# Expert lookup of a two-block transformer layer: experts in token-block order, routing placed between the row products

## Chip, cores, metric

One core of a Trainium2 chip runs the whole program. The metric is the device time of one execution in microseconds (us); the kernel before took 1429.31 us (median of 3 runs, 1425.92 to 1430.74).

## What is computed

Two blocks of a model run on 256 tokens of width 1024. All but the last stage (a mixer of attention, a recurrence and a convolution, twice; then a second block with its own mixers) is left alone by the change. The last stage is `peer`, a product-key mixture of 16384 experts, 8 heads, 16 experts per head and token:

```python
def one(xb):                                     # xb: a block of 128 tokens
    q = (xb @ w_pq).reshape(PEER_BLOCK, PEER_HEADS, 2, PEER_DKH)
    s = jnp.einsum('thpd,hpkd->thpk', q, sub_keys).astype(jnp.float32)
    sv, si = lax.top_k(s, PEER_TOPK)
    cand = (sv[:, :, 0, :, None] + sv[:, :, 1, None, :]).reshape(PEER_BLOCK, PEER_HEADS, -1)
    cidx = (si[:, :, 0, :, None] * N_KEYS + si[:, :, 1, None, :]).reshape(PEER_BLOCK, PEER_HEADS, -1)
    best, pos = lax.top_k(cand, PEER_TOPK)
    eidx = jnp.take_along_axis(cidx, pos, axis=-1)
    g = jax.nn.softmax(best, axis=-1)
    act = jax.nn.gelu(jnp.einsum('thkd,td->thk', expert_u[eidx], xb).astype(jnp.float32), approximate=False)
    return jnp.einsum('thk,thkd->td', (g * act).astype(xb.dtype), expert_v[eidx])
```

Its result, times a gate vector, is added to the residual and is the output.

## The kernel before

The program is written as a list of engine instructions; a scheduler turns it into one fixed order per engine at build time. `at(us)` sets the priority of what follows (lower goes first), but whatever is ready in the scheduler's own estimate may go ahead. On the chip each engine then runs its list in that order and waits where an operand or a buffer isn't ready. Tiles come from pools: `mk(..., tag, bufs=n)` means that n buffers of that name go round, and a new one waits for the release of an old one.

`peer` works on the two token blocks b = 0, 1 (128 tokens each, one per partition) and the heads h = 0 to 7:

- `scores(h)`: two weight tiles of 512 KB come in (`wpq`, issued on SP's queue), each is split by ACT into a rounded part `wh` (L323) and by DVE into the rest `wl` (L268), PE multiplies (48 matmuls), ACT copies the result to `qs` (L1480), and 4 matmuls give `sp`, a PSUM tile of the scores of both blocks. There are three buffers each for `wh` and `wl`, and two for `sp`.
- `routing(h, b)`: some 28 small DVE instructions, all in a chain: the top 16 of two rows of 128 scores (`top16`, L1464 to L1469, which reads `sp` in PSUM), 256 sums `cand`, their top 16, and from the positions the expert numbers `eix` (one-hot rows `oh`, a sum `ij`, L1521). ACT makes the exponentials of the softmax (L1526) in the middle; DVE then needs its sum for a reciprocal (L1527).
- `experts(h, b)`: for each of 16 experts POOL issues one gather (L1556): 128 rows of 8 KB, one per token, holding both `expert_u` and `expert_v`, into a buffer `G` of 8 KB per partition. DVE makes the row product (L1559): `G` times `hn[b]`, summed over 1024 columns. After a chunk of `CH` = 4 experts ACT applies Gelu (L1561), DVE multiplies with the softmax weights into `w` (L268), ACT makes four diagonal matrices `dg` (L1566, three buffers), and PE adds each expert's second half to two PSUM accumulators per block (`c`, `o` for block 0, `t`, `acx` for block 1). When PE has read a `G`, its buffer is free for another gather. There are `NG` = 11 of them.
- ACT loads a table whenever it goes from Gelu to the exponential or back.
- Eight more weight tiles (`wada`) are summed on DVE into `gs` (L262, `modsum`) for the gate vector `gtb`. At the end DVE multiplies the accumulators with it and adds the residual, and four transfers write the output.

Order of work before: head by head, block 0 then block 1 of each head (`for h ... for b ...: experts(h, b, ...)`). All calls of `scores` and `routing` stand ahead of the experts in the program with priorities spread over the stage; the scheduler takes them as soon as they are ready.

Of the kernel before, what the change touches and what calls it, by code (L numbers as in the profile page):

```python
# [240 lines left out]
def program(tc, A, dbg=lambda *a: None, stop=99):  # L241
# [1200 lines left out]
    def peer(B):  # L1442
# [17 lines left out]
        gat = [mk(pp, [128, 8, 16], tag=f"gat{b}") for b in range(2)]  # L1460
        io16 = C("iota")[:, None, 0:16].broadcast_to([128, 32, 16])

        def top16(v, ix, src, n):
# [4 lines left out]
            dve.max(v[:, 8:16], w)
            dve.max_index(ix[:, 8:16], v[:, 8:16], w)  # L1469

        def scores(h, t):
# [13 lines left out]
            return sp  # L1485
# [11 lines left out]
        def routing(h, b, sp):  # L1497
# [15 lines left out]
            sif = mk(pp, [128, 2, 16], tag="sif", bufs=2)
            dve.tensor_copy(sif, si)
            oh = mk(pp, [128, 2, 16, 16], tag="oh", bufs=1)
            of = oh.rearrange("p w k c -> p (w k) c")
            tt(of, io16, pf.rearrange("p w k -> p (w k)")[:, :, None].broadcast_to([128, 32, 16]), ALU.is_equal)
            for w in range(2):
                tt(oh[:, w], oh[:, w], sif[:, w, None, :].broadcast_to([128, 16, 16]), mul)
            ij = mk(pp, [128, 2, 16], tag="ij", bufs=2)  # L1520
            dve.tensor_reduce(ij.rearrange("p w k -> p (w k)"), of, axis=AX.X, op=add)  # L1521
            stt(eix[b][:, h], ij[:, 0], 128.0, ij[:, 1], mul, add)
# [19 lines left out]
        CH = 4  # L1542
        vacc = []

        def experts(h, b, t):
# [3 lines left out]
            for c in range(0, 16, CH):  # L1549
# [26 lines left out]
        for b in range(2):  # L1576
            routing(0, b, sps[0])
# [68 lines left out]
```

## Time and profile before

| | |
|---|---|
| median of 3 runs | 1429.31 us |
| the profiled execution: its own time / span in the profile | 1432.05 us / 1430.3 us |
| busy: PE / DVE / ACT / POOL | 86% / 69% / 36% / 21% of the span |
| gathers (queue q0): bytes, share of the 16 DMA engines | 268.45 MB, 46.0% of the span |
| mean granted TensorE clock | 0.924 |

The span runs from the first to the last instruction. The profile cuts it into 40 slices of 35.8 us; `peer` takes the last 20 of them (the first gather is issued at 725.8 us). "Idle before" of an instruction names what ended the wait. A DMA's time to landing is counted from its issue. PEclk is the clock granted to TensorE, 1.00 for 2.4 GHz and 0.50 for 1.2 GHz.

### The profile page before, as it was taken

The page shows a single profiled execution, that of the slowest core. Times are in us where ns is not written, and L with a number is a line of the kernel's source. Part 1 is how long each engine was busy: PE and PEld are TensorE (multiplying, and loading weights), DVE is VectorE, ACT ScalarE, POOL GpSimd, SP SyncE. Part 2 cuts the span into 40 slices and gives each one's busy share as a digit, 9 for nine tenths or more (in the row PEclk, how much of TensorE's full clock was granted, in tenths as well). Part 3 has the DMA queues.
Part 4 walks back from the last instruction along what each step waited for, and adds up shares of the span by engine and source line. Part 5 has one row for each costly group of instructions (what it writes and reads, how often), then busy time and mean ns, then how long its engine had stood idle before and what let it go on. Part 6 is the DMA issues. An engine that isn't in the chain of part 4 may idle for free.

```text
span 1430.3 us, 17866 instructions
## 1 busy us (share of the span) xinstructions
PE 1226.4 (86%) x6050; PEld 805.5 (56%) x6050; DVE 981.7 (69%) x2452; ACT 519.0 (36%) x1116; POOL 307.3 (21%) x279
## 2 busy tenths in 40 slices
PE   6999899999889999999897677788787877878786
PEld 5988568789759888658785333333333333333332
DVE  6898855699977673556689999955555545455554
ACT  5536643445755553454533334311111111111111
POOL 0000000000000000000032344454454444434450
PEclk9999999899999997989998789899999899998999
DMA  8677547556314341401379799999999999999994
GB/s 322 202 273 259 176 136 249 162 171 231 118 38 129 123 126 59 133 0 45 133 313 422 273 350 344 372 420 422 422 422 421 422 421 422 421 421 421 422 421 201
DMA packets 71339, 387.50 MB, mean 271 GB/s; under 512 B 8401, under 2 KB 9425, under 8 KB 38226
## 3 DMA queue, kind: packets, MB, share of 16 engines
q0 software_dynamic: 36864, 268.45, 46.0%
q1 hardware_dynamic: 34386, 117.93, 24.5%
q8 instruction: 48, 0.79, 0.2%
q14 instruction: 41, 0.34, 0.1%
HBM read 385.30 MB, written 1.05 MB: 270 GB/s over the span
## 4 chain that ended last, share of the span: by engine, by line
PE 48%; DMA 21%; DVE 14%; issue 9%; POOL 5%; ACT 2%; POOLq 0%; SPq 0%; DVEq 0%; ACTq 0%
PE acc L256 22%; DMA G<-uv,eix 18%; PE acx L256 10%; PE s L256 5%; DVE G L1559 5%; POOL G L1556 5%; PE t L256 2%; DMA wm<-wada 2%; PE o L256 2%; PE c L963 2%; DVE oh L268 1%; PE s L412 1%; PE c L256 1%; PE t L259 1%; DVE tmp L1467 1%
## 5 line engine op out<-in xcount | busy, mean ns | idle before, releaser
L1559 DVE SCALAR_TENSOR_TENSOR G<-G,hn 128x1024 f32<-128x1024 f32 x256 | 313.9, 1227 | 224.9 <-DMA G<-uv,eix 215.3
L1556 POOL DMA_INDIRECT G<-uv,eix x256 | 300.0, 1172 | 393.3 <-PE o L256 146.3
L323 ACT ACTIVATE wh<-w 128x1024 fp32r<-128x1024 f32 (+2 forms) x142 | 148.6, 1048 | 204.3 <-PE acc L256 124.9
L268 DVE TENSOR_TENSOR wl<-w,wh 128x1024 fp32r<-128x1024 f32 (+2 forms) x142 | 171.7, 1212 | 62.7 <-ACT wh L323 61.7
L256 PE MATMUL t<-G,dg 128*128 128x512 f32 x256 | 150.0, 671 | 68.5 <-ACT dg L1566 68.5
L256 PE MATMUL c<-G,dg 128*128 128x512 f32 x256 | 147.9, 662 | 65.0 <-ACT dg L1566 65.0
L256 PE MATMUL acc<-hh,wh 128*128 128x256 f32 x608 | 178.6, 297 | 7.9 <-ACT hh L468 3.6
L256 PE MATMUL acc<-hh,wl 128*128 128x256 f32 x608 | 180.4, 299 | 2.0 <-DVE wl L268 2.0
L256 PE MATMUL acc<-hl,wh 128*128 128x256 f32 x608 | 168.3, 291 | 3.7 <-issue 2.1
L1566 ACT ACTIVATE dg<-cst,w 128x128 f32<-128x128 f32 x256 | 89.8, 394 | 161.4 <-PE acx L256 72.7
L256 PE MATMUL acx<-G,dg 128*128 128x512 f32 x256 | 143.5, 645 | 0.0
L256 PE MATMUL o<-G,dg 128*128 128x512 f32 x256 | 142.5, 641 | 0.0
L256 PEld LDWEIGHTS t<-G,dg 128*128 128x128 f32 x256 | 51.3, 211 | 146.5 <-ACT dg L1566 91.8
L1561 ACT ACTIVATE s<-s 128x4 f32<-128x4 f32 x64 | 13.2, 205 | 326.4 <-DVE G L1559 326.4
L256 PEld LDWEIGHTS acc<-hh,wh 128*128 128x128 f32 x608 | 121.5, 200 | 14.5 <-issue 4.5
L256 PEld LDWEIGHTS c<-G,dg 128*128 128x128 f32 x256 | 50.5, 209 | 139.9 <-ACT dg L1566 88.4
L256 PEld LDWEIGHTS acc<-hh,wl 128*128 128x128 f32 x608 | 122.1, 201 | 9.6 <-issue 5.2
L256 PEld LDWEIGHTS acc<-hl,wh 128*128 128x128 f32 x608 | 116.0, 197 | 5.8 <-issue 3.4
L262 DVE SCALAR_TENSOR_TENSOR g<-lu,pb,g 128x256 f32<-128x256 f32 x264 | 115.7, 483 | 0.2
L256 PEld LDWEIGHTS acx<-G,dg 128*128 128x128 f32 x256 | 53.7, 210 | 71.1 <-issue 71.1
L256 PEld LDWEIGHTS o<-G,dg 128*128 128x128 f32 x256 | 53.0, 207 | 69.9 <-issue 69.9
L1054 POOL MEMSET lu<- 128x16 f32 x1 | 0.2, 180 | 400.5 <-ACT onat L840 400.5
(493 smaller groups left out, 2003.3 us busy)
## 6 DMA issues: line engine op xcount, KB each, us to landing
w<-w SPq DMA_DIRECT2D x64, 512.0 KB, 5.4
wm<-wada SPq DMA_DIRECT2D x40, 512.0 KB, 4.2
wa<-cw SPq DMA_DIRECT2D x16, 512.0 KB, 4.1
w<-woa SPq DMA_DIRECT2D x16, 512.0 KB, 3.4
w<-wpq SPq DMA_DIRECT2D x16, 512.0 KB, 3.3
w<-w2t SPq DMA_DIRECT2D x12, 512.0 KB, 3.5
w<-wob SPq DMA_DIRECT2D x8, 512.0 KB, 4.3
w<-w2v SPq DMA_DIRECT2D x8, 512.0 KB, 3.8
```

The source lines that it names most:

```text
L256: pe.matmul(out, lhsT, rhs, start=start, stop=stop)
L259: pe.transpose(out, in_, ident)
L262: (e or dve).scalar_tensor_tensor(out, a, s, b, op0=op0, op1=op1)
L268: return (e or dve).tensor_tensor(out, a, b, op=op)
L323: act.activation(hi, w, AF.Copy)
L412: pe.matmul(acc[j:j + 32], ones[:, 0:32], sq[:, q] if square else srcs[i + q], start=i + q < 4, stop=i + q >= n - 4, tile_position=(0, j))
L963: pe.matmul(acc[32 * j:32 * j + 32], sc[:, k], w[:, j], start=k == 0, stop=k == 7, tile_position=(0, 32 * j))
L1467: dve.match_replace(w, v[:, 0:8], src, -3e38)
L1556: pool.indirect_dma_start(out=G, out_offset=None, in_=A["uv"], in_offset=bass.IndirectOffsetOnAxis(ap=eix[b][:, h, c + j:c + j + 1], axis=0))
L1559: dve.scalar_tensor_tensor(G[:, 0:D], G[:, 0:D], 1.0, hn[b], op0=mul, op1=mul, accum_out=s[:, j:j + 1])
L1561: act.activation(s, s, AF.Gelu)
L1566: act.activation(dg, ident, AF.Copy, scale=w[:, j:j + 1])
```

## The change

1. Experts go block by block: round r = 0 to 15 is head r % 8 of block r // 8.
2. `routing` becomes a generator that gives out one instruction at a time. Round r is given the routing of round r + 2 (round 0 those of rounds 1 and 2), and behind each row product `nside` of its instructions are pinned on DVE: 2, in round 0 4. Only `routing(0, 0)` runs ahead of the first gather.
3. `scores` copies its result from PSUM to `sca`, an SBUF tile for all heads (16 KB per partition), with one more ACT instruction per head; `routing` reads that. `scores(r + 2)` stands with round r.
4. The sums for the gate vector go in the same way from round 3 on; the output of block 0 from round 10 on, in a buffer of `G`; that of block 1 at the end.
5. The last round's chunks are 4, 4, 4, 2, 1, 1 rather than four of 4.
6. `NG` goes from 11 to 9, `cand` from two buffers to one, `PICK` (spacing of the priorities) from 2.6 to 2.5.

```diff
-        def routing(h, b, sp):
+        def routing(h, b):
+
+            def top16(v, ix, src, n):
+                w = mk(pp, [128, n], tag="tmp", bufs=2)
+                yield dve.max(v[:, 0:8], src)
...
-                top16(sv[:, p], si[:, p], sp[:, b, p], 128)
...
+                yield from top16(sv[:, p], si[:, p], sca[:, h, b, p], 128)
...
-            return sp
+            act.activation(sca[:, h], sp, AF.Copy)
...
+                    dot = dve.scalar_tensor_tensor(G[:, 0:D], G[:, 0:D], 1.0, hn[b], op0=mul, op1=mul,
+                                                   accum_out=s[:, j:j + 1])
                     rows.append(G)
...
+                    with tc.issue_after(dot.ins):
+                        for _ in range(nside):
+                            while side and next(side[0], 0) == 0:
+                                side.pop(0)
...
-        PICK, NG = 2.6, 11
+        PICK, NG = 2.5, 9
...
+        for r in range(16):
+            nxt = [routing(q % 8, q // 8) for q in ((1, 2) if r == 0 else (r + 2,)) if q < 16]
+            side[0:0] = nxt
+            if r == 3:
+                side.append(gate_sums())
+            if r == 10:
+                side.append(finish(0))
+            if r < 6:
+                scores(r + 2, U0 + 16 * PICK * r - 12)
+            experts(r % 8, r // 8, U0 + 16 * PICK * r, 4 if r == 0 else 2, (4, 4, 4, 4) if r < 15 else (4, 4, 4, 2, 1, 1))
+            at(U0 + 16 * PICK * (r + 1))
+            while side and (side[0] in nxt or r in (6, 12)):
+                for _ in side.pop(0):
+                    pass
```

How it stands on DVE. First, two row products that follow each other among the first 16 experts of the kernel before (the product is the row with `hn`; `eix`, `best`, `sv`, `si`, `pos` and `gat` belong to routing, `gs` to the gate sums):

```order
L1559 SCALAR_TENSOR_TENSOR G_8616,s_8609<-G_8616,hn_1231_7173 128x1024
L262 SCALAR_TENSOR_TENSOR eix_1233_7175<-ij_7630 128x16
L1468 MAX best_7654<-tmp_7658 128x8
L1468 MAX sv_7749<-tmp_7753 128x8
L262 SCALAR_TENSOR_TENSOR gs_8476<-w_8491,sc_19_102,gs_8476 128x1024
L1465 MAX_INDEX si_7750<-sv_7749,s_7744 128x8
L1469 MAX_INDEX pos_7655<-best_7654,tmp_7658 128x8
L265 TENSOR_SCALAR gat_1236_7178<-best_7654 128x16
L1469 MAX_INDEX si_7750<-sv_7749,tmp_7753 128x8
L1559 SCALAR_TENSOR_TENSOR G_8619,s_8609<-G_8619,hn_1231_7173 128x1024
```

and of the kernel after, in round 1:

```order
L1562 SCALAR_TENSOR_TENSOR G_7830,s_7829<-G_7830,hn_1231_7173 128x1024
L1497 MAX sv_7789<-tmp_7803 128x8
L1498 MAX_INDEX si_7790<-sv_7789,tmp_7803 128x8
L1562 SCALAR_TENSOR_TENSOR G_7835,s_7829<-G_7835,hn_1231_7173 128x1024
L268 TENSOR_TENSOR cand_7838<-sv_7789 128x256
L1494 MAX best_7840<-cand_7838 128x8
L1562 SCALAR_TENSOR_TENSOR G_7844,s_7829<-G_7844,hn_1231_7173 128x1024
L1495 MAX_INDEX pos_7841<-best_7840,cand_7838 128x8
L1496 MATCH_REPLACE tmp_7842<-best_7840,cand_7838 128x256
L1562 SCALAR_TENSOR_TENSOR G_7849,s_7829<-G_7849,hn_1231_7173 128x1024
```

Eight instructions, of three routings and of the gate sums, stood between two products; now there are two of one routing.

Second, DVE just ahead of the first gather, which needs `eix`, in the kernel before (`wl` are the splits for later heads, `ij` the last sum ahead of `eix`):

```order
L268 TENSOR_TENSOR wl_7686<-w_7682,wh_7684 128x1024
L1469 MAX_INDEX si_7291<-sv_7290,tmp_7300 128x8
L268 TENSOR_TENSOR cand_7304<-sv_7290 128x256
L268 TENSOR_TENSOR oh_7278<-oh_7278,sif_7276 128x256 x2
L1514 CAST sif_7319<-si_7291 128x32
L1464 MAX best_7306<-cand_7304 128x8
L268 TENSOR_TENSOR wl_7716<-w_7712,wh_7714 128x1024
L1521 TENSOR_REDUCE ij_7282<-oh_7278 128x32
L1464 MAX sv_7441<-s_7436 128x8
L1465 MAX_INDEX pos_7307<-best_7306,cand_7304 128x8
L1467 MATCH_REPLACE tmp_7310<-best_7306,cand_7304 128x256
L262 SCALAR_TENSOR_TENSOR eix_1233_7175<-ij_7282 128x16
```

and after:

```order
L268 TENSOR_TENSOR oh_7280<-cst_62,pf_7276 128x512
L268 TENSOR_TENSOR wl_7464<-w_7460,wh_7462 128x1024
L1529 RECIPROCAL sm_7288<-sm_7288 128x1
L268 TENSOR_TENSOR oh_7280<-oh_7280,sif_7278 128x256 x2
L265 TENSOR_SCALAR gat_1235_7177<-gat_1235_7177,sm_7288 128x16
L1523 TENSOR_REDUCE ij_7284<-oh_7280 128x32
L268 TENSOR_TENSOR wl_7721<-w_7717,wh_7719 128x1024
L262 SCALAR_TENSOR_TENSOR eix_1233_7175<-ij_7284 128x16
```

The other routings are gone from this stretch; two splits still stand ahead of `eix`.

Third, the end of DVE's list before, from the last chunk but one on (`w` is the chunk's weights, `t` and `acx` the accumulators of block 1):

```order
L268 TENSOR_TENSOR w_2182_10511<-s_10497,gat_1236_7178 128x4
L1559 SCALAR_TENSOR_TENSOR G_10530,s_10529<-G_10530,hn_1232_7174 128x1024
L1559 SCALAR_TENSOR_TENSOR G_10533,s_10529<-G_10533,hn_1232_7174 128x1024
L1559 SCALAR_TENSOR_TENSOR G_10536,s_10529<-G_10536,hn_1232_7174 128x1024
L1559 SCALAR_TENSOR_TENSOR G_10539,s_10529<-G_10539,hn_1232_7174 128x1024
L268 TENSOR_TENSOR w_2192_10543<-s_10529,gat_1236_7178 128x4
L268 TENSOR_TENSOR G_10561<-t_8511,gtb_8475 128x512
```

and after:

```order
L268 TENSOR_TENSOR w_2184_10527<-s_10513,gat_1236_7178 128x4
L1562 SCALAR_TENSOR_TENSOR G_10546,s_10545<-G_10546,hn_1232_7174 128x1024
L1562 SCALAR_TENSOR_TENSOR G_10549,s_10545<-G_10549,hn_1232_7174 128x1024
L268 TENSOR_TENSOR w_2192_10553<-s_10545,gat_1236_7178 128x2
L1562 SCALAR_TENSOR_TENSOR G_10564,s_10563<-G_10564,hn_1232_7174 128x1024
L268 TENSOR_TENSOR w_2197_10568<-s_10563,gat_1236_7178 128x1
L1562 SCALAR_TENSOR_TENSOR G_10575,s_10574<-G_10575,hn_1232_7174 128x1024
L268 TENSOR_TENSOR w_2201_10579<-s_10574,gat_1236_7178 128x1
L268 TENSOR_TENSOR G_10585<-t_7500,gtb_7425 128x512
```

The last four experts had one `w` behind all of them; now the first two have one, and the last two one each.

## Rows read from the trace of the kernel before

**Rows 1.** Page, part 2: busy tenths of DVE in 40 slices, and GB/s.

```profile
DVE  6898855699977673556689999955555545455554
...
GB/s 322 202 273 259 176 136 249 162 171 231 118 38 129 123 126 59 133 0 45 133 313 422 273 350 344 372 420 422 422 422 421 422 421 422 421 421 421 422 421 201
```

**Rows 2.** Windows of `peer`: from:to, us, busy (x instructions), clock, DMA share, GB/s.

```profile
728.00:780.00 52.00, 44.59 (x261) 35.88 (x259) 46.46 (x149) 17.57 (x30) 20.03 (x18) 0.93 1.01 418
780.00:920.00 140.00, 102.12 (x212) 44.72 (x212) 138.14 (x514) 52.82 (x106) 57.32 (x44) 0.82 0.88 333
920.00:1408.00 488.00, 386.04 (x790) 158.98 (x791) 253.67 (x450) 80.45 (x250) 220.76 (x194) 0.92 1.01 421
```

**Rows 3.** Groups by line and form, 780 to 920 us: DVE and POOL.

```profile
L1559 DVE SCALAR_TENSOR_TENSOR G<-G,hn 128x1024 f32<-128x1024 f32 x45 | 55.6, 1238 | 0.0
L268 DVE TENSOR_TENSOR oh<-cst,pf 128x512 f32<-128x512 f32 x12 | 8.6, 713 | 0.0
L262 DVE SCALAR_TENSOR_TENSOR gs<-w,sc,gs 128x1024 f32<-128x1024 f32 x6 | 8.1, 1348 | 0.0
L1556 POOL DMA_INDIRECT G<-uv,eix x44 | 58.8, 1336 | 86.5 <-PE acx L256 18.5 <-PE o L256 14.3 <-DVE ij L1521 13.6
```

**Rows 4.** Waits, longest in total first: of 780 to 920 us, then of 920 to 1400 us.

```profile
ACT gat L1526 <- DVE gat L265: 31.0, 8, 12.6
...
DVE G L1559 <- DMA G<-uv,eix: 209.2, 181, 1.7
```

**Rows 5.** DVE, POOL and ACT in order of time ahead of the first row product.

```profile
707.76 0.60 ACT L1480 ACTIVATE qs<-acc 128x512 f32<-128x512 f32 x1 [1.82 <-PE acc L256]
...
710.48 0.29 DVE L1464 MAX8 sv<-s 128x8 f32<-128x128 f32 x1
...
725.34 0.18 DVE L262 SCALAR_TENSOR_TENSOR eix<-ij 128x16 uint32<-128x16 f32 x1
...
725.81 1.08 POOL L1556 DMA_INDIRECT G<-uv,eix  x1 [20.38 <-DVE eix L262]
727.19 1.01 POOL L1556 DMA_INDIRECT G<-uv,eix  x1 [0.30 <-issue]
```

**Rows 6.** All gathers, line L1556: durations, and time from issue to landing.

```profile
L1556 POOL DMA_INDIRECT G<-uv,eix x256: 932/938/2275, 725.8 to 1397.8; - x128
...
DMA to landing us min/median/max: 6.7/16.1/17.1
```

**Rows 7.** DVE in order of time, one chunk of the later part: a chunk's last product, the weights behind it.

```profile
1292.98 1.23 DVE L1559 SCALAR_TENSOR_TENSOR G<-G,hn 128x1024 f32<-128x1024 f32 x1 [1.27 <-DMA G<-uv,eix]
...
1294.49 0.16 DVE L268 TENSOR_TENSOR w<-s,gat 128x4 f32<-128x4 f32 x1 [0.27 <-ACT s L1561]
...
1302.93 1.23 DVE L1559 SCALAR_TENSOR_TENSOR G<-G,hn 128x1024 f32<-128x1024 f32 x1 [1.26 <-DMA G<-uv,eix]
```

**Rows 8.** PE in order of time: a chunk at full clock, then the start of one at the lower.

```profile
1285.24 1.13 PE L256 MATMUL c<-G,dg 128*128 128x512 f32 x2 [2.82 <-ACT dg L1566]
...
1291.35 1.02 PE L256 MATMUL o<-G,dg 128*128 128x512 f32 x2
1295.20 2.07 PE L256 MATMUL c<-G,dg 128*128 128x512 f32 x2 [2.82 <-ACT dg L1566]
...
1301.80 1.02 PE L256 MATMUL c<-G,dg 128*128 128x512 f32 x2
```

**Rows 9.** Windows of 4 us: first and last of 17 dips of the clock after 940 us.

```profile
984.00:988.00 4.00, 3.33 (x4) 1.51 (x5) 1.94 (x4) 0.99 (x3) 0.00 (x0) 0.50 1.01 422
1376.00:1380.00 4.00, 4.00 (x6) 1.54 (x5) 2.37 (x4) 0.57 (x2) 1.13 (x1) 0.57 1.01 420
```

**Rows 10.** The end, in order of time: last product, Gelu, first and last matmul pair, last addition.

```profile
1414.24 1.23 DVE L1559 SCALAR_TENSOR_TENSOR G<-G,hn 128x1024 f32<-128x1024 f32 x1 [1.23 <-DMA G<-uv,eix]
...
1416.46 1.13 PE L256 MATMUL t<-G,dg 128*128 128x512 f32 x2 [3.97 <-ACT dg L1566]
...
1424.27 1.02 PE L256 MATMUL acx<-G,dg 128*128 128x512 f32 x2
1424.47 0.69 DVE L268 TENSOR_TENSOR G<-t,gtb 128x512 f32<-128x512 f32 x1 [8.56 <-PE t L256]
```

More of the change, by code (lines that the diff above doesn't have):

```diff
@@ L1505, in routing @@
             best = mk(pp, [128, 16], tag="best", bufs=2)
             pos = mk(pp, [128, 16], U32, tag="pos", bufs=2)
-            top16(best, pos, cand.rearrange("p a b -> p (a b)"), 256)
+            yield from top16(best, pos, cand.rearrange("p a b -> p (a b)"), 256)
             pi = mk(pp, [128, 2, 16], U32, tag="pi", bufs=2)
-            ts(pi[:, 0], pos, 4, None, ALU.logical_shift_right)
-            ts(pi[:, 1], pos, 15, None, ALU.bitwise_and)
+            yield ts(pi[:, 0], pos, 4, None, ALU.logical_shift_right)
@@ L1518, in routing @@
             for w in range(2):
[L1519 removed]
+                yield tt(oh[:, w], oh[:, w], sif[:, w, None, :].broadcast_to([128, 16, 16]), mul)
             ij = mk(pp, [128, 2, 16], tag="ij", bufs=2)
[L1521 to L1522 removed]
+            yield dve.tensor_reduce(ij.rearrange("p w k -> p (w k)"), of, axis=AX.X, op=add)
@@ L1523, in routing @@
+            yield stt(eix[b][:, h], ij[:, 0], 128.0, ij[:, 1], mul, add)
             g = gat[b][:, h]
-            ts(g, best, best[:, 0:1], None, sub)
+            yield ts(g, best, best[:, 0:1], None, sub)
             sm = mk(pp, [128, 1], tag="sm", bufs=2)
             act.activation(g, g, AF.Exp, accum_out=sm)
-            dve.reciprocal(sm, sm)
-            ts(g, g, sm, None, mul)
+            yield dve.reciprocal(sm, sm)
+            yield ts(g, g, sm, None, mul)
         xn = XT.rearrange("p k t -> p (k t)").rearrange("p (b d) -> p b d", b=2)
@@ L1569, in experts @@
                            h == 7 and c + j == 15)
-        PICK, NG = 2.6, 11
+                c += n
+        PICK, NG = 2.5, 9
         U0 = B + 22
-        sps = {}
-        sps[0] = scores(0, B)
+        scores(0, B)
         at(B + 8)
-        for b in range(2):
-            routing(0, b, sps[0])
+        for _ in routing(0, 0):
+            pass
         at(B + 5.5)
         natural()
-        for h in range(1, 8):
-            sp = scores(h, U0 + 32 * PICK * (h - 1) - 8)
-            for b in range(2):
-                at(U0 + 32 * PICK * (h - 1) + 6 + 16 * PICK * b)
-                routing(h, b, sp)
+        scores(1, B + 9)
         at(B + 16)
```

84 lines of the change are left out of this document (44 added, 40 removed).

## The prediction

> **What bounds the kernel now.** I read the page's slices first. In the last 20 of 40 slices the kernel gathers experts: from slice 27 on it moves 420 to 422 GB/s in every slice but the last, which is the transfers' own limit, while DVE is half busy. Four slices ahead of that (23 to 26) show 273 to 372 GB/s with DVE at 9 tenths [rows 1]. The windows give sizes. From 728 us on, when gathers are under way, 418 x 52 + 333 x 140 + 421 x 488 = 21.7 + 46.6 + 205.4 = 273.8 MB are moved in 680 us; at 421 GB/s they take 650 us. Nearly all of the difference lies in 780 to 920 us: 46.6 MB want 110.7 us and took 140, so **29.3 us are lost there** [rows 2].
>
> Who loses them is seen in the groups and waits of that stretch. DVE works 138.1 of 140 us [rows 2] and gets through 45 row products, where a gather every 2.49 us (a chunk of four takes 1302.93 - 1292.98 = 9.95 us [rows 7]) would ask for 56. Besides the products it did 12 routings and 6 gate sums [rows 3]. The chain behind a product is ACT, PE, and then POOL, which has no free buffer: ACT waited 31.0 us, once 12.6 us, for a routing's softmax on DVE, with the Gelu of a chunk queued behind it; PE then has no diagonal matrices, frees no `G`, and POOL issues nothing. After 920 us, when all routing is done, it is the products that wait for gathers, 209.2 us in all [rows 4]: the transfers set the pace.
>
> So the stage has a floor: first issue, plus 650 us of transfers, plus a tail. The change can save the 29.3 us, part of the start and part of the tail, and can lose by making the transfers wait anew.
>
> **Routing between the products.** It is all kept, only spread. In the crowded stretch 138.1 - 55.6 (products) - 8.1 (sums) leaves 74.4 us for 12 routings, 6.2 us each [rows 2, 3]. A round takes 16 x 2.49 = 39.8 us and now holds 16 x 1.24 = 19.8 us of products, 6.2 us of routing and four `w` of 0.16 us [rows 3, 7]: 27 us, 67%. In early rounds two splits of a weight tile come on top (1024 columns, so about a product each, 2.5 us), in rounds 3 to 6 two gate sums each (2.7 us [rows 3]), still below 33 us. Round 0 holds two routings and more splits, about 36 us. DVE therefore keeps up everywhere, and two routing instructions (the longest, 0.71 us [rows 3]) behind a product fit in the 1.25 us that DVE is idle ahead of the next one [rows 7]. The lost 29.3 us go: **-29.3**.
>
> **New waits on DVE.** The reciprocal and the last multiplication of a routing stand in DVE's list with products behind them, and wait for ACT's exponential, which stands behind other ACT work. The trace shows no such wait of any length; from below it is 0, from above I take the 12.6 us that ACT waited for DVE at this very place [rows 4]. With a product between the subtraction and the reciprocal (round 0 has none) I take it as hidden, except in round 0. The splits wait for PE in the same way; there the first nine gathers (22 us of transfers) cover them.
>
> **The start.** `eix` came 14.9 us after routing's first instruction [rows 5], which shared DVE with another routing and splits. Now 6.2 us of routing, two splits (2.5 us) and one more ACT copy of 512 columns (0.60 us as `qs` [rows 5]) make 9.3 us, 5.5 us less: the one end. The other is that the second split, which stands ahead of `eix`, waits until PE has let go of an earlier head's buffer, and the start is later by 1 us than before. I take **-2**.
>
> **Nine buffers for eleven.** This is the part that can hurt. Measured from the landing of a chunk's last row, PE starts 2.22 us later (1292.98 to 1295.20 [rows 7, 8]), with two routing instructions ahead of `w` some 2.8. A row takes PE 4 x 0.43 = 1.72 us at full clock, since eight pieces of 0.86 us make a chunk [rows 8]. The chunk's first row landed 3 x 2.49 = 7.5 us earlier and is free 2.8 + 1.7 = 4.5 us later; the ninth gather after it is due 9 x 2.49 = 22.4 us after it landed. That leaves 22.4 - 7.5 - 4.5 = **10.4 us** from issue to landing, where the quickest landing took 6.7 us; the usual 16.1 us are a queue of 6.5 gathers behind eleven buffers [rows 6]. When the granted clock is at the lower level, as at the start of the second chunk shown, two rows take 6.6 us [rows 8]; the second, landed 5.0 us earlier, is free after 9.4 us and leaves 8.0 us. 17 such dips lie in the 46 chunks after 940 us [rows 9]. Both are above 6.7, by 3.7 and 1.3 us, so the queue stays filled, with little to spare. The output of block 0 holds one buffer for a while in round 10 (8 buffers: 2.5 us less). For slips in dips, in round 0 and there I take **+4** together, between 0 and the rivals below.
>
> **The tail.** The last product starts at 1414.24, PE begins at 1416.46 and DVE's final additions at 1424.47, 10.2 us after that product [rows 10]. Now PE is through with the third chunk 0.8 us ahead of the last product (its twelfth row lands 10 us earlier, then 2.2 + 6.9), then does rows 13 and 14 until 2.6 us after it, row 15 until 4.3, row 16 until 6.1: **-4**, with ends of -2 (no dip before either, and a gap) and -6.
>
> **GpSimd's issues.** An issue takes 0.938 us in the median, in the crowded stretch 1.336 on average, at most 2.275, with 0.30 us between two [rows 3, 5, 6]. DVE at 70% lies between these stretches; an issue stays below 2.49 us and costs nothing. The Trainium skill, "SBUF — State Buffer", section "SBUF: two separate sides", says that while DVE runs certain copies, casts and scalar operations GpSimd is locked out of a shared port and cannot write its descriptors, so that the transfers starve. That speaks against putting such instructions behind every product. By the row the sum is unchanged; by the rule it is that of rival 4.
>
> **Sum.** The profiled execution took 1432.05 us of its own (span 1430.3). 1432.05 - 29.3 - 2 - 4 + 4 = 1400.75; it lies 2.74 us above the median of the runs shown, so 1398.0 us is forecast; without any new loss 1394.
>
> **Rivals.**
> 1. *Round 0 stalls.* One wait as long as the 12.6 us [rows 4], of DVE for ACT or of a split for PE, comes into the open before the queue is built up: 1398 + 12.6 = 1411. For: round 0's DVE list is 90% full. Against: nine gathers are then queued.
> 2. *Slow-clock chunks run dry.* If a gather in the running stage needs 9 us instead of 6.7, chunks with a dip lose 1 us each: 17 of 46, so 24 of 64: 1394 + 24 = 1418.
> 3. *Nine buffers hold up every chunk, and it gets slower.* A row's buffer goes round 256 / 9 = 28.4 times; each us by which issue to landing exceeds 10.4 costs 28.4 us. The gain of 35 us (1429 to 1394) is gone from 11.6 us on. At 13.2 us, halfway to the usual 16.1, it is 2.8 x 28.4 = 80 us: 1474. For: nothing but the median [rows 6]. Against: the least landing time.
> 4. *GpSimd can't issue.* If every issue took the longest time seen, 2.275 + 0.30 = 2.575 us [rows 5, 6], it would exceed a gather's 2.49 by 0.09 us for the 224 gathers of rounds 0 to 13: 20 us, 1418. This is what the rule on the shared port would come to; the row of 1.336 us speaks against it.
> 5. *The gap stays.* The transfers are held up by something other than DVE's routing (the weight tiles that come in at the same time, say): 1398 + 29.3 = 1427. Against: the bytes of those tiles are in the 333 GB/s.
>
> **How the numbers follow.** Chances: forecast 0.63, rivals in turn 0.12, 0.06, 0.08, 0.04, 0.07. The range: below, start and tail at their good ends and no loss, 1394 - 3.5 - 2 = 1389; above it takes in rival 1 and reaches to 1416, the edge of 2 and 4. Some 0.3%, 4.3 us, is what a measurement here tells from no change. Faster by more: forecast, 1, 2, 4 and a little of 5, 0.87; slower: 3, 0.08; the rest is the same.
>
> **What would show it.** Right: GB/s of 415 or more in every window from shortly after the first gather to the end, DVE at about two thirds in the routing rounds, landing times near 16.1 - 2 x 2.49 = 11 us in the median, the first issue at 722 to 726 us, some 12 us from the last product's start to the end rather than 16. Wrong: DVE's products no longer waiting for gathers while POOL waits for PE and GB/s fall below 400 chunk by chunk (rivals 2, 3); issues of more than 2 us as a rule (4); a hole in the first 60 us after the first gather (1).

## The result, and the profile after

| | kernel after | kernel before, on the same chip |
|---|---|---|
| median (range, runs) | 1406.53 us (1404.60 to 1406.84, 4) | 1427.62 us (1424.73 to 1430.74, 4) |
| ratio, 95% interval | 0.9849 (0.9824 to 0.9874) | |
| second measurement (e10) | 1406.09 us (1403.03 to 1410.13, 5) | 1426.78 us (1422.77 to 1432.15, 17) |
| ratio, 95% interval | 0.9864 (0.9839 to 0.9889) | |

The change is faster by 1.5%, about 21 us. The forecast was 1398.0 us, 31 us faster than 1429.31; the time lies 8.5 us above it and inside its range.

How the profiled executions differ (1432.05 us before, 1406.54 after), cut at two events that every trace shows, the issue of the first gather and the start of the last row product:

| | before | after | difference | forecast |
|---|---|---|---|---|
| issue of the first gather | 725.81 | 723.70 | -2.1 | -2 |
| from there to the last product | 688.4 | 669.6 | -18.9 | -29.3 + 4 = -25.3 |
| from there to the span's end | 16.1 | 11.3 | -4.7 | -4 |
| own time less span | 1.75 | 1.94 | +0.2 | 0 |

So one line is off, by 6.4 us. The four lines add up to 25.5 us, 4.4 more than the medians differ by, because the profiled execution of before lies that far above its median and that of after lies on it. Below, the middle stretch is called *the stage*.

The page of after, part 2 (busy tenths of DVE and GB/s in 40 slices), against [rows 1]: the four poor slices 23 to 26 are full, and from slice 23 to 37 DVE is level at 6 to 7 tenths. New is a poor slice, the 28th (349).

```profile
DVE  6898865599987674455768766777676767667554
...
GB/s 323 193 282 263 168 162 218 169 170 245 133 21 108 165 98 75 132 33 1 151 193 423 421 422 421 421 407 349 421 422 412 422 421 413 414 422 421 417 409 273
```

The windows of after, columns as in [rows 2]:

```profile
728.00:780.00 52.00, 47.50 (x257) 34.49 (x256) 41.90 (x117) 21.43 (x39) 18.58 (x18) 0.97 1.01 421
780.00:920.00 140.00, 110.94 (x239) 46.48 (x238) 99.28 (x252) 32.52 (x84) 61.54 (x55) 0.93 1.01 422
920.00:1380.00 460.00, 359.06 (x772) 152.23 (x771) 312.22 (x770) 103.92 (x270) 197.87 (x179) 0.92 1.00 412
```

780 to 920 us went from 333 to 422 GB/s, DVE from 138.1 to 99.3 of 140 us (71%). From 920 us on the rate is 412 where it was 421: by bytes, (421.5 - 412) / 421.5 x 460 = 10.4 us are lost there.

The groups of after in 780 to 920 us, against [rows 3]: 54 products rather than 45, which now wait for gathers, and GpSimd issues in 1.135 us on average (1.336 before).

```profile
L1562 DVE SCALAR_TENSOR_TENSOR G<-G,hn 128x1024 f32<-128x1024 f32 x54 | 66.1, 1224 | 38.3 <-DMA G<-uv,eix 37.6 <-PE o L256 0.7
```
```profile
L1559 POOL DMA_INDIRECT G<-uv,eix x55 | 62.4, 1135 | 78.6 <-PE o L256 55.5 <-DVE tmp L1496 10.5 <-DVE G L1562 5.6
```

All gathers of after, against [rows 6]:

```profile
L1559 POOL DMA_INDIRECT G<-uv,eix x256: 932/938/1983, 723.7 to 1383.2; - x128
...
DMA to landing us min/median/max: 8.2/11.9/20.9
```

**The hole.** Three windows of after, then its timeline there (start, us, engine, line, operation, in brackets the idle time before it):

```profile
920.00:940.00 20.00, 14.08 (x48) 7.88 (x47) 15.76 (x39) 3.62 (x10) 6.73 (x6) 0.89 1.02 422
940.00:960.00 20.00, 17.16 (x56) 9.30 (x56) 14.00 (x31) 6.07 (x12) 6.24 (x6) 0.85 0.80 290
960.00:980.00 20.00, 17.58 (x41) 7.29 (x39) 14.14 (x41) 4.38 (x12) 12.16 (x10) 1.00 1.00 399
```
```profile
777.97 123.11 SPq L314 DMA_DIRECT2D w<-wada  x4
903.36 0.33 SPq L314 DMA_DIRECT2D w<-wpq  x1
...
940.86 0.40 ACT L1575 ACTIVATE dg<-cst,w 128x128 f32<-128x128 f32 x1 [3.48 <-PE o L256]
...
947.84 0.60 ACT L1473 ACTIVATE qs<-acc 128x512 f32<-128x512 f32 x1 [4.96 <-PE acc L256]
950.45 0.60 ACT L1478 ACTIVATE sca<-s 128x512 f32<-128x512 f32 x1 [2.01 <-PE s L256]
...
952.36 0.21 ACT L1566 ACTIVATE s<-s 128x4 f32<-128x4 f32 x1
...
961.04 0.60 ACT L1606 ACTIVATE gtb<-s 128x512 f32<-128x512 f32 x1 [3.83 <-PE s L256]
...
962.39 0.20 ACT L1566 ACTIVATE s<-s 128x4 f32<-128x4 f32 x1
```
```profile
941.04 0.94 POOL L1559 DMA_INDIRECT G<-uv,eix  x1 [7.41 <-PE o L256]
...
949.80 0.94 POOL L1559 DMA_INDIRECT G<-uv,eix  x1 [3.27 <-PE o L256]
956.99 0.94 POOL L1559 DMA_INDIRECT G<-uv,eix  x1 [6.25 <-DVE tmp L1496]
```

Read from the last fence back: POOL, without a free buffer, stands still for 7.4, 3.3 and 6.3 us. ACT waits 4.96 us for PE with `qs` of head 7, 2.01 us with `sca`, and only then applies Gelu (L1566) to a chunk whose products were done earlier; 10 us later the two `gtb` copies stand ahead of Gelu in the same way. Head 7 is so late because its weight tiles (`wpq`) stand in SP's queue behind `wada` tiles, which hold the buffers `w` until the gate sums read them: the queue stood for 123 us. The first of the three stops has another part in it. PE runs at the lower clock there and takes longer to let go of the buffers:

```profile
936.00:942.00 6.00, 5.45 (x8) 2.62 (x9) 4.11 (x8) 2.50 (x6) 0.94 (x1) 0.50 1.01 419
```

How much of the hole is this dip's, no run separates.

The start of after, against [rows 5] (first instruction of routing, `eix`, first issue):

```profile
712.44 0.49 DVE L1494 MAX8 sv<-sca 128x8 f32<-128x128 f32 x2 [1.11 <-ACT sca L1478]
...
722.54 0.17 DVE L262 SCALAR_TENSOR_TENSOR eix<-ij 128x16 uint32<-128x16 f32 x1
...
723.70 1.08 POOL L1559 DMA_INDIRECT G<-uv,eix  x1 [66.88 <-PE acc L256]
```

The end of after, against [rows 10] (last product, first of the final additions):

```profile
1393.26 1.23 DVE L1562 SCALAR_TENSOR_TENSOR G<-G,hn 128x1024 f32<-128x1024 f32 x1 [0.79 <-DMA G<-uv,eix]
...
1398.76 0.69 DVE L268 TENSOR_TENSOR G<-t,gtb 128x512 f32<-128x512 f32 x1 [3.84 <-PE t L256]
```

### The profile page after: what moved, and what is told of

The parts are those of the page before. It is cut to its first block, busy times and chain, and to the rows that moved or that the text cites. A ratio compares the mean times of both kernels' runs of the same rounds, so it can differ in the third digit from the quotient of the medians.

```text
span 1404.6 us, 17908 instructions
## 1 busy us (share of the span) xinstructions
PE 1214.2 (86%) x6050; PEld 798.9 (57%) x6050; DVE 995.6 (71%) x2454; ACT 528.6 (38%) x1130; POOL 291.9 (21%) x279
## 4 chain that ended last, share of the span: by engine, by line
PE 49%; DMA 27%; DVE 8%; issue 8%; POOL 5%; ACT 2%; POOLq 0%; DVEq 0%; SPq 0%; ACTq 0%
DMA G<-uv,eix 24%; PE acc L256 22%; PE acx L256 11%; PE s L256 6%; POOL G L1559 5%; DVE G L1562 4%; PE t L256 3%; PE o L256 2%; DMA wm<-wada 2%; PE c L963 2%; PE s L412 1%; DMA w<-wpq 1%; PE t L259 1%; PE c L256 1%; PE o L645 1%
## 5 line engine op out<-in xcount | busy, mean ns | idle before, releaser
L1559 POOL DMA_INDIRECT G<-uv,eix x256 | 284.4, 1111 | 443.0 <-PE o L256 134.4
L256 PE MATMUL t<-G,dg 128*128 128x512 f32 x256 | 146.7, 657 | 69.6 <-ACT dg L1575 69.6
L256 PE MATMUL acc<-hh,wh 128*128 128x256 f32 x608 | 178.5, 297 | 11.4 <-ACT wh L323 4.3
L1566 ACT ACTIVATE s<-s 128x4 f32<-128x4 f32 (+1 forms) x66 | 13.5, 205 | 331.8 <-DVE G L1562 331.7
```

Source lines behind the costliest of these rows:

```text
L256: pe.matmul(out, lhsT, rhs, start=start, stop=stop)
L1559: pool.indirect_dma_start(out=G, out_offset=None, in_=A["uv"], in_offset=bass.IndirectOffsetOnAxis(ap=eix[b][:, h, k:k + 1], axis=0))
L1566: act.activation(s[:, 0:n], s[:, 0:n], AF.Gelu)
```

## Experiments

All runs in one table. "Stage" is from the first gather's issue to the last product's start, "end" from there to the span's end, both of the profiled execution; GB/s of 780 to 920 and of 920 to 1340 us; "alone" is the number of whole us, after the rate has fallen at the end, with a DMA share of 0.04 to 0.10 (left blank where it was not read).

| | median us | ratio to before (95%) | GB/s | GB/s | stage us | end us | alone us |
|---|---|---|---|---|---|---|---|
| before | | 1 | 333 | 422 | 688.4 | 16.1 | 3 |
| after | 1406.53 | 0.9849 (0.9824 to 0.9874) | 422 | 412 | 669.6 | 11.3 | 1 |
| e10, after again | 1406.09 | 0.9864 (0.9839 to 0.9889) | 421 | 411 | 670.2 | 11.4 | 1 |
| e1, gate sums late | 1405.69 | 0.9820 (0.9798 to 0.9843) | 417 | 413 | 671.7 | 12.8 | |
| e2, eight buffers | 1445.89 | 1.0105 (1.0072 to 1.0138) | 394 | 389 | 706.7 | 12.9 | |
| e3, last chunks of 4 | 1409.23 | 0.9842 (0.9815 to 0.9870) | 419 | 411 | 671.9 | 14.4 | 1 |
| e4, not pinned | 1430.06 | 0.9993 (0.9974 to 1.0012) | 321 | 417 | 698.5 | 12.9 | |
| e5, chunks of 2 | 1400.33 | 0.9815 (0.9793 to 0.9838) | 421 | 418 | 668.1 | 9.4 | 6 |
| e6, ten buffers | 1403.58 | 0.9845 (0.9821 to 0.9870) | 421 | 417 | 666.4 | 12.7 | 4 |
| e7, heads, eleven | 1398.46 | 0.9802 (0.9781 to 0.9823) | 421 | 418 | 666.7 | 10.1 | 5 |
| e8, chunks of 2, eight | 1398.12 | 0.9813 (0.9784 to 0.9842) | 420 | 417 | 667.4 | 9.4 | 4 |
| e9, before with nine | 1433.36 | 1.0042 (1.0022 to 1.0062) | 326 | 419 | 692.2 | 14.3 | |
| e11, heads, 2, eleven | 1397.31 | 0.9795 (0.9770 to 0.9820) | 421 | 421 | 667.1 | 9.4 | 8 |
| e12, blocks, 2, ten | 1397.71 | 0.9790 (0.9767 to 0.9814) | 421 | 421 | 666.8 | 9.4 | 8 |

**e4: is it the pinning that fills the 780 to 920 us?**

```diff
-                    with tc.issue_after(dot.ins):
+                    if True:
                         for _ in range(nside):
```

> One edit to the kernel after: the instructions of routing, the gate sums and block 0's output are written at the same places, but not tied behind the row products, so that the scheduler takes them as soon as they are ready, as in the kernel before. Experts still go block by block with nine buffers. Theory A (the spreading of routing recovers the 29.3 us): DVE is full again in the first 200 us of the gathers, the transfers fall to 340 GB/s or less there, and with nine buffers a little more than 29 us is lost: 1406.5 + 29 to 45 = 1436 to 1452 us. Theory B (block order, which lets routing of block 1 come late, does it by itself): 1405 to 1412 us.

The window of e4, DVE full again, in block order and with everything else as after:

```profile
780.00:920.00 140.00, 99.97 (x237) 44.85 (x235) 138.69 (x522) 52.77 (x104) 56.33 (x44) 0.87 0.85 321
```

The stage is 28.9 us longer than that of after, and the ratio is 0.9993: without the pinning the whole change is worth nothing. That is theory A in mechanism, though its time (1436 to 1452) was missed by 6 us: the profiled execution took 1436.43, but it is the slowest of ten, whose median is 1430. The edit lets the gate sums go as well as routing; the two are not separated.

**e2 and e8: how near the edge are nine buffers, and an edge of what?**

```diff
-        PICK, NG = 2.5, 9
+        PICK, NG = 2.5, 8
```

> One edit to the kernel after: NG = 8 for 9, so each gather is issued 2.49 us later against its turn. By the prediction's working nine buffers leave 10.4 us from issue to landing, 8.0 in a chunk at the lower clock; eight leave 7.9 and 5.5. Theory A (a gather alone needs about 6.7 us): only chunks at the lower clock run dry, 1.2 us each in some 24 chunks of 64, and the hole at 936 to 964 grows by 2.5: 1406.5 + 29 + 2.5 = 1438 us. Theory B (the margin was larger than worked out): the hole alone grows, 1409 us. Theory C (a gather in the running stage needs the 8.2 us that was the least in the kernel after, or more): every chunk loses, 256 / 8 = 32 turns of a buffer with 0.3 us or more on top of A: 1448 us or more.

Two windows of e2:

```profile
780.00:920.00 140.00, 106.12 (x203) 43.30 (x201) 94.00 (x240) 28.46 (x75) 58.16 (x52) 0.87 0.99 394
920.00:1340.00 420.00, 325.38 (x680) 138.66 (x681) 281.38 (x715) 94.79 (x240) 174.96 (x154) 0.88 0.98 389
```

The rate is low everywhere, not in a few chunks: between A and C. The stage grows by 37.1 us; a buffer goes round 256 / 8 = 32 times, so 1.2 us are missing at each turn, and nine buffers (2.49 us more) have 1.3 us to spare. e8 takes the same eight buffers with chunks of 2:

```diff
-            experts(r % 8, r // 8, U0 + 16 * PICK * r, 4 if r == 0 else 2, (4, 4, 4, 4) if r < 15 else (4, 4, 4, 2, 1, 1))
+            experts(r % 8, r // 8, U0 + 16 * PICK * r, 4 if r == 0 else 2, (2,) * 8 if r < 15 else (2,) * 7 + (1, 1))
```

> Chunks of 2 as in e5, with eight buffers. Theory A (issue to landing): 15.4 - 2.5 = 12.9 us are left, more than nine buffers with chunks of four have, so 1396 to 1404 us, where eight buffers with chunks of four took 1434 to 1456. Theory B (the number of gathers in flight itself sets the rate): about as slow as eight buffers with chunks of four, 1430 us or more.

The window of e8:

```profile
920.00:1340.00 420.00, 320.93 (x703) 128.21 (x701) 294.84 (x768) 105.98 (x293) 173.62 (x165) 0.98 1.01 417
```

Theory A: the loss of e2 is gone (stage 667.4). It is not the number of buffers that counts but the time that their turn leaves from issue to landing. The granted clock is also higher, 0.98 where e2 had 0.88, and a PE that is through sooner frees its buffers sooner; no run separates this from the shorter wait within a chunk.

**e1: does the hole come from head 7's late weights?**

```diff
-            if r == 3:
+            if r == 6:
                 side.append(gate_sums())
...
-            while side and (side[0] in nxt or r in (6, 12)):
+            while side and (side[0] in nxt or r in (8, 12)):
```

> One edit to the kernel after: the gate sums are begun in round 6 and ended in round 8 (there: 3 and 6), so that the eight tiles of wada come in behind all the weight tiles of scores and no longer hold the buffers that head 7's weights wait for. Theory A (late weights): the one hole of the kernel after (936 to 964 us, 7.5 us) comes from head 7's scores, done in round 5 only, whose copies and those of the gate vector stand on ACT ahead of a chunk's Gelu. Then the hole goes: 1406.5 - 7.5 = 1399 us, and no 20 us stretch after the first gathers is below 400 GB/s. Theory B (nine buffers are too few for anything out of the common, late weights or not): the splits of the early rounds get more crowded and the gate sums' own copies and flush still hit a chunk in rounds 6 to 8: the hole moves, 1404 to 1408 us.

The hole of 940 to 960 us is gone (420 GB/s). Four other windows of e1:

```profile
776.00:780.00 4.00, 4.00 (x11) 1.83 (x10) 2.57 (x7) 3.25 (x5) 1.99 (x2) 1.00 0.48 139
...
1020.00:1024.00 4.00, 3.88 (x10) 1.37 (x8) 3.96 (x7) 0.10 (x1) 2.92 (x3) 1.00 0.63 193
...
1076.00:1080.00 4.00, 4.00 (x10) 1.73 (x10) 2.37 (x11) 0.70 (x2) 2.89 (x2) 1.00 0.87 289
...
1184.00:1188.00 4.00, 4.00 (x7) 1.46 (x6) 2.02 (x5) 3.15 (x5) 0.99 (x2) 0.62 0.85 301
```

The weights came early, and the scores of two heads now hold ACT from 763 to 774 us; the gate sums and their copies follow at 1020 and 1076. The stage is 671.7 us, no shorter. Its ratio lies 0.3% below that of after, and the intervals overlap: whether e1 gains anything is open, that it does not gain 7.5 us in the stage is shown. Theory A is right that the hole comes from head 7's scores and the gate sums (the edit moves both, so their shares stay open), and theory B on what moving them is worth: with nine buffers, whatever is out of the common makes a hole where it is put.

**e5 and e6: more time from issue to landing, by chunks of 2 or by a tenth buffer.** e5 is the edit of e8 with nine buffers. In e6 block 0's scores, which are needed for two rounds only, make room:

```diff
-        PICK, NG = 2.5, 9
+        PICK, NG = 2.5, 10
...
-        sca = mk(pp, [128, 8, 2, 2, 128], tag="sca")
+        sca1 = mk(pp, [128, 8, 2, 128], tag="sca1")
+        sca0 = {}
...
+            sca0[h] = mk(pp, [128, 2, 128], tag="sca0", bufs=2)
...
```

> One edit to the kernel after: chunks of 2 experts in every round (last round: seven of 2, then 1 and 1), nine buffers. A chunk's first row then waits one gather for the Gelu (2.49 us) rather than three (7.5 us): by the prediction's working a buffer comes free 5.0 us earlier and leaves 15.4 us from issue to landing rather than 10.4. Theory A (what is lost after the first gathers, 10.4 us by the windows, is a shortage of time from issue to landing): the transfers run at 420 GB/s or more nearly throughout, 1406.5 - 8 to 10.4 = 1396 to 1399 us. Theory B (the loss is head-of-line blocking of ACT, which gets 61 more Gelu and PE more and shorter pieces, with the clock lower): 1406 us or more.

> The kernel after with NG = 10. The room comes from the scores of block 0, which are kept for two heads at a time rather than for all eight (6 KB), at the price of one more ACT copy per head in place of one twice as long. Each gather is issued 2.49 us earlier against its turn. Theory A (shortage of time from issue to landing; nine stand at the edge, since eight lost some 33 us): the hole at 936 to 964 shrinks by 2.5 us, the small ones at the lower clock go: 1406.5 - 5.5 = 1401 us. Theory B (the stop of POOL in round 5 is longer than any queue covers): 1404 to 1406 us.

e5 runs at 421 GB/s through the hole's place; its one stop is at block 0's output:

```profile
1180.00:1200.00 20.00, 13.15 (x27) 5.30 (x28) 15.18 (x38) 6.47 (x16) 8.39 (x7) 0.95 0.99 377
```

By bytes, e5 loses some 6 us less than after in 920 to 1340 us (418 GB/s rather than 412), yet its stage is only 1.5 us shorter and its end 1.9; by the ratios it gains 0.3%, 5 us (the intervals overlap), not the 8 to 10 of theory A. e6 has a shallower hole (369 GB/s in 940 to 960 us, 290 in after), a stage shorter by 3.2 us, and a ratio that can't be told from that of after. Both did to the transfers what theory A said, and most of it did not reach the end. Where it went is seen in e11, below.

**e7: pinning in the old order, with eleven buffers.** Head by head, `routing` reading PSUM, no `sca`. The gate sums go to rounds 12 to 14 and both outputs behind the last round; of the diff these lines matter most:

```diff
-                yield from top16(sv[:, p], si[:, p], sca[:, h, b, p], 128)
+                yield from top16(sv[:, p], si[:, p], sps[h][:, b, p], 128)
...
-        PICK, NG = 2.5, 9
+        PICK, NG = 2.5, 11
...
-            nxt = [routing(q % 8, q // 8) for q in ((1, 2) if r == 0 else (r + 2,)) if q < 16]
+            nxt = [routing(q // 2, q % 2) for q in ((1, 2) if r == 0 else (r + 2,)) if q < 16]
...
-            if r < 6:
-                scores(r + 2, U0 + 16 * PICK * r - 12)
+            if r % 2 and r < 12:
+                scores((r + 3) // 2, U0 + 16 * PICK * r - 12)
...
```

> The pinned routing with the order of the kernel before: head by head, block 0 then block 1, no copy of the scores to SBUF (routing reads PSUM), eleven buffers, scores of a new head every second round, the gate sums in rounds 12 to 14, both outputs at the end; last chunks 4, 4, 4, 2, 1, 1. Theory A (spreading the routing is what brings the 29.3 us, and nine buffers are what it costs): no window after the first gathers is below 415 GB/s, 1406.5 - 10.4 + 1.7 (block 0's output at the end) = 1398 us. Theory B (block order is needed: with scores in the middle of the running rounds to the end, chunks are held up in every second round): 1406 to 1415 us.

The ratio is 0.9802, the stage 666.7 us. Theory A: block order and the copies to SBUF are not needed for the gain; they cost two buffers. Its "no window below 415 GB/s" failed, though: 397 from 1300 to 1340 us, where the gate sums and their copies now stand. With eleven buffers they still make a dip.

**e9: nine buffers alone, in the kernel before.**

```diff
-        PICK, NG = 2.6, 11
+        PICK, NG = 2.6, 9
```

> One edit to the kernel before: NG = 9 for 11, nothing else of the change. Theory A (nine buffers stand at the edge, so that only work out of the common and chunks at the lower clock are lost): in 780 to 920 us, where DVE is full and held up chunks already, the stops grow by up to 2 x 2.49 us each for the two or three longest, and some 3 us go later, as in the kernel after: 1429 + 4 to 13 us. Theory B (nine are enough for anything): 1427 to 1431 us.

```profile
780.00:920.00 140.00, 99.57 (x214) 43.39 (x215) 138.05 (x517) 52.43 (x109) 54.14 (x44) 0.87 0.85 326
```

It is slower by 0.42% (0.22 to 0.62), 6 us: the window of e9 has 326 GB/s for 333, the stage 692.2 us for 688.4. Theory A.

**e3: what shortens the end?** The last round in chunks of 4:

```diff
-            experts(r % 8, r // 8, U0 + 16 * PICK * r, 4 if r == 0 else 2, (4, 4, 4, 4) if r < 15 else (4, 4, 4, 2, 1, 1))
+            experts(r % 8, r // 8, U0 + 16 * PICK * r, 4 if r == 0 else 2, (4, 4, 4, 4))
```

> One edit to the kernel after: the last round's chunks are 4, 4, 4, 4 as before the change. From the last product's start to the end it took 16.1 us before and 11.3 after. Theory A: the smaller chunks are the reason, the four pieces of PE's work come back behind the last product: 1406.5 + 4.7 = 1411 us. Theory B: the output of block 0, which the kernel after no longer has at the end, is the reason (two transfers and four DVE instructions of 0.69 us fewer there): 1406.5 + 1 to 2 = 1408 us.

The end of e3, last product and first of the final additions:

```profile
1395.03 1.23 DVE L1562 SCALAR_TENSOR_TENSOR G<-G,hn 128x1024 f32<-128x1024 f32 x1 [1.19 <-DMA G<-uv,eix]
...
1403.56 0.69 DVE L268 TENSOR_TENSOR G<-t,gtb 128x512 f32<-128x512 f32 x1 [6.86 <-PE t L256]
```

There are 8.5 us between the two where after has 5.5; the end takes 14.4 us for 11.3 (after) and 16.1 (before). So some 3 of the 4.7 us are the chunks'. The other 1.7 are not the output of block 0, since the kernel before had that behind it well ahead of its last product (1414.24):

```profile
1399.40 0.69 DVE L268 TENSOR_TENSOR G<-c,gtb 128x512 f32<-128x512 f32 x1
```

And e9, the kernel before with nine buffers, ends as e3 does, 8.53 us from the one row to the other and 14.3 in all:

```profile
1417.90 1.23 DVE L1559 SCALAR_TENSOR_TENSOR G<-G,hn 128x1024 f32<-128x1024 f32 x1 [1.85 <-DMA G<-uv,eix]
...
1426.43 0.69 DVE L268 TENSOR_TENSOR G<-t,gtb 128x512 f32<-128x512 f32 x1 [6.86 <-PE t L256]
```

What differs is the clock behind the last product, in order before and e9:

```profile
1414.00:1420.00 6.00, 3.54 (x6) 1.52 (x7) 1.40 (x3) 1.59 (x5) 0.00 (x0) 0.79 0.00 0
```
```profile
1418.00:1424.00 6.00, 5.65 (x14) 2.28 (x13) 1.30 (x3) 1.59 (x5) 0.00 (x0) 1.00 0.00 0
```

So theory B is wrong, and the 1.7 us are a dip of the clock in the one profiled execution of before. The 3 us are not firm either: with the same last chunks as after, e1, e2, e4 and e6 ended in 12.7 to 12.9 us. The timing cannot tell 3 us here (1403 to 1411 us).

**e10, e11, e12: after again, and the two ways to give the gathers time, put together.** e10 is after, unchanged; e11 is e7 with e5's chunks; e12 is e6 with e5's chunks and e1's late sums.

> The kernel after, unchanged, on the same chip as the other runs of this group: 0.985 of the kernel before, 1402 to 1410 us. From the first gather's issue to the end it should take 681 us again, with a hole near 936 to 964 us in every execution, since the hole comes from the order of the instructions and not from chance.

> Head by head with pinned routing and eleven buffers as in e7, with chunks of 2 as in e5. Theory A (both act by the time from issue to landing, so together there is little left to gain): from the first issue to the end some 674 us, where the kernel after took 681, e7 676.8 and e5 677.5; a time of 1394 to 1400 us. Theory B (they act on different things and add up): 672 us or less, 1390 to 1393 us.

> Block by block with chunks of 2, ten buffers (as e6) and the gate sums in rounds 6 to 8 (as e1). Theory A: with that much time from issue to landing neither head 7's scores, the gate sums nor block 0's output make a stretch of 20 us below 410 GB/s; some 674 us from the first issue to the end, 1394 to 1400 us. Theory B (block 0's output holds DVE, not a buffer): a dip to some 375 GB/s near 1180 us stays, 677 us.

e10 shows the hole again (315 GB/s in 940 to 960 us) and the stage within 0.6 us. e11 and e12 have no stop left (in windows of 20 us from 740 to 1360 us 419 to 424 GB/s in e11, 415 to 423 in e12) and beat both kernels: 0.9790 for e12, 0.7% below e10 on the same chip. By the time theory A (1397 us); but from the first issue to the end they took 676.5 and 676.2 us, not 674, and their stage of 667 us is that of e6, e7 and e8, which do have stops. The end of the transfers says why. In order: before, after, e11.

```profile
1408.00:1412.00 4.00, 4.00 (x11) 1.71 (x9) 1.46 (x3) 0.00 (x0) 0.00 (x0) 1.00 0.56 231
1412.00:1416.00 4.00, 0.49 (x2) 0.00 (x0) 2.41 (x5) 0.21 (x1) 0.00 (x0) 1.00 0.02 10
```
```profile
1388.00:1392.00 4.00, 4.00 (x10) 1.74 (x10) 2.59 (x5) 1.07 (x4) 0.00 (x0) 1.00 0.74 307
1392.00:1396.00 4.00, 4.00 (x11) 1.73 (x10) 1.59 (x6) 1.21 (x4) 0.00 (x0) 1.00 0.01 4
```
```profile
1372.00:1376.00 4.00, 3.57 (x9) 1.30 (x8) 2.15 (x3) 0.10 (x1) 0.00 (x0) 1.00 0.72 292
1376.00:1380.00 4.00, 2.80 (x7) 1.37 (x8) 1.61 (x5) 0.90 (x3) 0.00 (x0) 1.00 0.09 35
1380.00:1384.00 4.00, 2.16 (x6) 0.75 (x5) 2.39 (x4) 0.90 (x3) 0.00 (x0) 1.00 0.06 27
```

In e11 the rate falls at 1376 us, and then 25 to 35 GB/s go on for 8 us at a share of 0.06 to 0.09: 1/16 is 0.0625, one DMA engine of the sixteen. It works off what it is behind, and each of the last gathers waits for it; the last three products start at 1380.53, 1383.00 and 1385.47, 2.47 us apart as in the running stage. In the trace its packets stand one behind another there, for each gather eight rows of 8 KB, 0.31 us each, and one of 4 bytes that reports them. In after, with its stops, there is next to nothing of this.

The trace shows how far behind this engine is all along. A gather is reported by sixteen such signals, one from each engine, and has landed with the last. The time from the fifteenth signal to the sixteenth, in us, as the median of twenty gathers (of sixteen in the last column; a gather counts if all its signals are in the trace, 245 of 256 in after, 255 or 256 in the others):

| gathers | 20 to 39 | 60 to 79 | 80 to 99 | 160 to 179 | 180 to 199 | 240 to 255 |
|---|---|---|---|---|---|---|
| after | 0.0 | 1.9 | 0.3 | 0.7 | 0.2 | 1.0 |
| e6 | 0.4 | 2.2 | 0.2 | 1.2 | 2.0 | 3.9 |
| e5 | 0.8 | 2.5 | 3.5 | 5.4 | 4.3 | 6.1 |
| e11 | 0.5 | 2.4 | 3.1 | 5.5 | 6.1 | 8.2 |

Where nothing stops, the lag grows to the end (e11). A stop takes it away: across the hole it falls from 1.9 to 0.0 us in after (gathers 80 to 84) and from 2.2 to 0.2 in e6 (85 to 88), across block 0's output from 5.9 to 3.4 in e5 (175 to 185).

## Why the prediction was right, and where not

- **The 29.3 us of 780 to 920.** Right as a mechanism: DVE's routing held up the transfers there, and placing it between the products brings 333 to 422 GB/s; e4 takes the pinning away (from the gate sums too) and has 321. DVE's share came to 71% where 67% was worked out.
- **The floor is the step that failed**: "420 to 422 GB/s ... which is the transfers' own limit", and with it "at 421 GB/s they take 650 us". It made the stage 688.4 - 29.3 = 659.1 us without any loss. Six kernels with quite different stops, from none (e11, e12) to those of e6 (417 GB/s from 920 on), all have a stage of 666.4 to 668.1 us. 421 GB/s is what sixteen engines move together while all have work; a gather has landed when the last of them is done, and one runs behind. What fifteen lose in a stop of a few us, the sixteenth uses to catch up: the table of lags shows its lag gone or smaller behind the stops, and in the table of runs "alone" falls as the stops grow (8, 8, 6, 5, 4, 4, 1 us) while the stage hardly changes. So some 8 of the 29.3 us could not be had in this way.
- **The new loss**, +4 in the sum, came to 669.6 - 667 = 2.6 us in the stage, though 10.4 us of transfers by the windows: its place was wrong. It was not dips of the clock alone, nor round 0 or the output of block 0, but in the main the scores of head 7 and the gate sums, 7 us of bytes, with one dip among them; the queue of SP with `wada` ahead of `wpq` was not looked at. The floor's 7.9 us less these 1.4 are the 6.5 us by which the stage is off; that is the same 669.6 us parted at 667, and proves nothing more. The +4 came near for the wrong reasons, which is luck.
- **The last 2.7 us**: the forecast took off 2.74 because the profiled execution of before lay above its median. That of after lies on its own (1406.54 and 1406.53); such a correction is within what executions of one kernel scatter here (before: 1423 to 1432 in one group of runs). With the 6.4 us of the stage, less 0.6 of the other lines, it makes up the 8.5 us by which the forecast was off.
- **Nine buffers.** The 10.4 us left, against 6.7 needed, gave 3.7 us to spare at full clock and 1.3 in a chunk at the lower; e2 gives 1.3 on average (37.1 us over 32 turns, taken from 2.49). Landing 11.9 us in the median, 11 forecast. Rival 3 (every chunk held up) is what happens at eight: it stood one buffer away.
- **The start.** `eix` comes 10.1 us after routing's first instruction (9.3 forecast, 14.9 before), but that begins 2 us later, after the new copy, and the issue follows `eix` by 1.2 us rather than 0.5. -2.1 is what was taken; one execution doesn't prove it, since after and e10, the same program, issue their first gather at 723.7 and 719.6 us.
- **New waits on DVE**, put at nothing, are small: in the stage DVE waited ten times for the exponential, 10.2 us in all and at most 2.6, far from the upper bound of 12.6.

```profile
DVE sm L1529 <- ACT gat L1528: 10.2, 10, 2.6
```

- **The end**: -4.7 for -4, but at most 3 us of it by the chunks. The rest is that the profiled execution of before had a dip of the clock behind its last product (0.79, where e3 and e9 have 1.00), 1.7 us that went into the -4, though its lower end, -2, allowed for no dip. That the sum came so near is in part luck.
- **The rivals.** 1: no stop in the first 60 us after the first gather (421 GB/s). 2: at most in part (the hole's first stop). 3: no. 4: issues of 1.135 us where a 71% busy DVE stands beside them, 0.938 in the median of the whole, at most 1.983. The Trainium skill's rule that certain DVE instructions keep GpSimd from writing descriptors ("SBUF — State Buffer", section "SBUF: two separate sides") costs nothing here: beside a DVE that is 52% busy (before, 920 to 1400 us) an issue took 1.139 us on average, and only the full DVE of 780 to 920 us stood beside 1.336. 5: no.

The rule that did bear on the floor was another. The Trainium skill, "DMA: Bandwidth & Descriptors", section "Latency and other measured facts", says that two of the sixteen DMA engines are usually slower than the rest in traces, and supposes that the GpSimd queue's descriptors are the cause. The rows of e11 agree in that an engine runs behind, but one engine's share is left over and not two; which engine it is, no run here shows, and the cause that the Trainium skill supposes is not what the trace points to (see the last section).

## What to carry to other kernels

A rate in a window is no floor when a transfer is spread over many engines: look at the last few us of transfers, at the share there, before a gap in the rate is counted as time to be won. When buffers are taken for something else, work out the time that their turn leaves from issue to landing, including how long a row waits for the rest of its chunk: halving the chunk gave as much as two buffers (eight with chunks of 2 have the stage of ten with chunks of 4). Work that is out of the common (a late weight tile, a copy on an engine with an ordered list) costs a hole wherever that margin is small, so give it margin rather than move it. Before a stretch of one profiled execution is priced, look at its granted clock in other runs: 1.7 us of the tail here were a dip.

## What the hardware showed that was not expected

- One DMA engine's worth of work is left for up to 8 us when the stage never stops (above). Its lag grows in steps. After 800 us there are ten of 0.95 to 1.01 us in e11 and ten of 0.93 to 0.98 in e12, 53 to 78 us apart, and each is seen at a gather that lands 2.0 to 2.4 us after the start of an 8 KB packet on q14, a queue that the page of the profile lists as one for instructions:

```profile
q14 instruction: 43, 0.35, 0.1%
```

  That loading instructions is what holds this engine up is inferred from these twenty coincidences. In either run 8 of the 18 such packets after 800 us come without a step, and why a packet of 0.33 us should cost 0.96 is not shown.
- With chunks of 2 TensorE is granted more: mean clock 0.97 to 0.98 from 920 to 1340 us (e5, e8, e11, e12) where after has 0.92, with shorter idle times between its pieces (its longest wait for `dg` ahead of `t` was 2.3 us in e5, 3.8 in after).
- More buffers do not let GpSimd run ahead without end. In e11, where buffers are free early, the issues wait for landings of gathers, 190 times, 230.6 us in all:

```profile
L1559 POOL DMA_INDIRECT G<-uv,eix x256: 933/1342/1998, 718.4 to 1365.2; - x128
...
  DMA G<-uv,eix: 230.6, 190
...
DMA to landing us min/median/max: 6.7/19.1/26.5
```

At 19.1 us from issue to landing and a gather every 2.49 us some 7.7 are under way, an estimate. This is the program's own limit and tells nothing of the depth of a hardware queue: the gathers signal on eight semaphores in turn, and in the trace 186 of the 190 waits end with the landing of the gather eight before, on the semaphore that the new one is to use again. Beyond eight under way more buffers can't help this program. An issue took 1.34 us in the median there, 0.94 in after. Those of e11 that waited for something else took 1.27, so that it is not this wait alone that makes them longer, and the cause stays open.
